# GpSimd adds the weights for the seven products, which cover all four column groups; operands at constant places mod 256

## The chip, the cores and the metric

One core of a Trainium2 chip runs the whole program. The metric is device time in microseconds (us), lower is better. Engines: TensorE (PE; PEld is its weight load), VectorE (DVE), ScalarE (ACT), GpSimd (POOL), and SyncE (SP), which issues the loads.

## The reference

One decoder layer in fp32: a sequence of 256 tokens behind 16 meta tokens, model width 2048, MLP width 8192.

```python
u = rmsnorm(h, g_mix);  proj = u @ w_in          # 2048 -> 6144
o_diff = diff_attention(...);  o_sb = stick_breaking_attention(...)
h = h + concat(o_diff, o_sb) @ w_out              # 2048 -> 2048
m = rmsnorm(h, g_mlp)
hid = square(relu(m @ w_up))                      # 2048 -> 8192
h = h + hid @ w_down                              # 8192 -> 2048
```

## The kernel before

**Products.** Each fp32 product is made of three matmuls in a rounded format (fp32r): hi x hi, hi x lo and lo x hi, where hi is the rounded value and lo the rest. `triple` issues the three. A weight tile comes from memory as a *raw* tile, 128 x 4 x 256 fp32 (512 KB), on SP's queue, into one of five raw buffers. ACT casts it (`whi`, L179) and DVE subtracts (`wlo`, L181). The results go into weight buffers, of which the MLP has five, used in turn along `order`: the split of item g waits until item g - 5 has been used by PE. The split runs four items ahead.

**The MLP.** The hidden width is cut into 8 rounds of 1024 columns. In a round, PE makes the hidden columns of the *next* round ("up", 16 items) and the share of the present one in the output ("down"). The output is 2048 wide, in four column groups u of 512; a *unit* (r, u) is one column group of one round, with four weight tiles p = 0 to 3. The letters in the code are items of PE's order:

- c: one up tile, 24 matmuls with 256 moving columns.
- d: one plain down tile, 12 matmuls of 512 columns.
- a and b: one down tile in the form with seven products in place of eight (a Strassen-like scheme on 2 x 2 blocks; the units in `FAST`). "a" makes three products from three quarters of the raw tile as they are (9 matmuls of 256, a cast and a subtraction of 768 wide). Then three additions overwrite parts of the raw tile with sums of its quarters (L295 with 512 columns, L297 and L299 with 256, all on DVE). "b" makes four products from the summed tile (12 matmuls of 256, split 1024 wide). A raw tile is free when b is split.

The seven products of a column group are summed over all rounds: at the end of a fast unit ACT copies the four PSUM banks to `Z[u]` (L930), and copies the next unit's `Z` back into its banks (L935) where one exists, bank by bank in the order 0, 1, 3, 2 (`fast_evac`; bank 3 is half-sized). At the last fast round of a column group its seven sums are combined. A plain unit's result is added to H by DVE (`plain_evac`). The hidden values need block sums of their own (three DVE operations in `up_evac`, L887 to L891), after ACT's relu and square; then they are cast (ACT, L897) and subtracted (DVE, L899) 1024 wide.

**What sets the order.** PE's order is the list `order`: for each round a string per column group. ACT's, DVE's and SP's instructions are written down by a planner, `Pace`, which keeps a model clock for each engine and lets a job go on when its inputs are there by that clock and the engine is at most 500 ns ahead of PE; each engine then runs its own list in that order, waiting where an input is late. Before, column groups 0, 1 and 2 are fast in rounds 0 to 6, and the four d of group 3 are spread over the units:

```python
for u, mix in ((0, "cdcabcabcabcab"), (1, "cdcabcabcabcab"), (2, "cdcabcabcdabccab")):
```

In the last round (no up left) only group 0 is fast.

**Places.** LINE is 16 fp32 (64 bytes). The pads and `offset` set at which address modulo 256 the operands lie: m, mixed, hid (moving or stationary) and the weight buffers' hi and lo.

Of the kernel before, what the change touches and what calls it, by code (L numbers as in the profile page):

```python
# [7 lines left out]
F32 = mybir.dt.float32  # L8
F32R = mybir.dt.float32r
AF = mybir.ActivationFunctionType  # L10
ALU = mybir.AluOpType
AX = mybir.AxisListType

P = 128
DM = 2048
SEQ = 256
META = 16
TOK = META + SEQ
KT = DM // P
EPS = 1e-6  # L20
NEG = -1e30
ROW = 576
LINE = 16
ROUNDS = 8
PAIRS = 4
# [5 lines left out]
MLP_PARTS = 5  # L31
MLP_LEAD = 4
MLP_PAD = 1
FAST = {(r, u) for r in range(ROUNDS - 1) for u in range(3)} | {(ROUNDS - 1, 0)}
PSUM_BANKS = {"acc": 4, "att": 4}
SLOTS = {"k": 4, "q": 4, "v": 2, "e": 3, "pr": 2, "ah": 2, "m": 2, "n": 2}
K0 = META + P
# [8 lines left out]
class Pace:  # L46
# [9 lines left out]
    QUEUE = 500.0  # L56

    def __init__(self, lanes):
        self.pe = self.dve = self.act = 0.0
        self.lanes = {n: ([], w) for n, w in lanes}  # L60
        self.at = {}
        self.banks = {}
# [9 lines left out]
    def A(self, n, after=0.0):  # L72
        self.act = max(self.act, self.pe, after) + n / 1.2 + 93
        return self.act + self.WAIT

    def job(self, lane, gen):
        self.lanes[lane][0].append([(0.0, None), gen])
# [16 lines left out]
    def pump(self):  # L94
        more = True
        while more:
            more = False
            for jobs, width in self.lanes.values():
                for job in jobs[:width]:
                    t, engine = job[0]  # L100
                    if t <= self.pe and {None: 0, "v": self.dve, "a": self.act}[engine] <= self.pe + self.QUEUE:
                        try:
                            job[0] = next(job[1])
                        except StopIteration:
                            jobs.remove(job)
                        more = True
                        break
                if more:
                    break
# [13 lines left out]
def hymba_layer(ctx: ExitStack, tc: tile.TileContext, xT_d, xh_d, win_d, wout_d, wup_d, wdn_d, cst_d, par_d, out_d):  # L123
    nc = tc.nc
    cp = ctx.enter_context(tc.tile_pool(name="const", bufs=1))
    big = ctx.enter_context(tc.tile_pool(name="big", bufs=1))
    wp = ctx.enter_context(tc.tile_pool(name="weights", bufs=1))
# [7 lines left out]
    pc = Pace((("fetch", 9), ("weights", 9), ("once", 2), ("evac", 6), ("head", 4)))  # L135
# [17 lines left out]
    def retile(tag, shape, name):  # L153
        return rtile(tag, shape, name, SLOTS["e"])

    def two_parts(x, k, n):

        return x[:, :, : k * n].rearrange("p a (k n) -> p k a n", n=n)


    par = cp.tile([P, G_END], F32, name="par")
    cst = tp.tile([P, C_ID], F32, bufs=1, name="cst")
# [1 line left out]
    xT = big.tile([P, KT, TOK], F32, tag="x", name="xT")  # L164
    big.tile([P, LINE], F32, name="pad_act")
    um = big.tile([P, KT, ROW], F32R, tag="act", name="u")[:, :, : 2 * TOK].rearrange("p k (a n) -> p k a n", a=2)
    big.tile([P, 2 * LINE], F32, name="pad_mix")
    mixed = two_parts(big.tile([P, 2, KT * SEQ + LINE], F32R, tag="mix", name="mixed"), KT, SEQ)

    def split_u(k):  # L170
        g = par[:, G_MIX + k : G_MIX + k + 1]
# [13 lines left out]
    strips = []  # L185
# [16 lines left out]
    def down(r, u, ps):  # L202
        return [(x, r, u, p) for p in ps for x in ("ab" if (r, u) in FAST else "a")]

    order += up(0, 0, range(3)) + up(0, 1, range(3)) + up(0, 0, (3,)) + up(0, 1, (3,)) + up(0, 2, range(4)) + up(0, 3, range(4))
    for r in range(ROUNDS - 1):
        c = iter([key for i in range(PAIRS) for key in up(r + 1, i, range(4))])
        d = iter(down(r, 3, range(PAIRS)))
        for u, mix in ((0, "cdcabcabcabcab"), (1, "cdcabcabcabcab"), (2, "cdcabcabcdabccab")):
            ab = iter(down(r, u, range(PAIRS)))  # L210
            order += [next({"c": c, "d": d, "a": ab, "b": ab}[x]) for x in mix]
        assert not [*c, *d]
    ab = iter(down(ROUNDS - 1, 0, range(PAIRS)))
    d = iter([key for u in (1, 2, 3) for key in down(ROUNDS - 1, u, range(PAIRS))])
    order += [next({"d": d, "a": ab, "b": ab}[x]) for x in "dd" + "adbd" * 4 + "dd"]
# [20 lines left out]
    def fetch(number, pieces=1):  # L236
        if number < len(loads):
            g = loads[number]
            if not raws:
                wp.tile([P, 3 * LINE], F32, name="pad_w")  # L240
            raws[g] = wp.tile([P, 4, 256], F32, tag="raw", bufs=RAW, name=f"raw_{g}")
            n = 4 // pieces
            for i in range(pieces):
                k = slice(n * i, n * i + n)
                raw_at[g, i] = load(raws[g][:, k], source(g)[:, k], n * 256)
                yield

    ring = {g: g - PARTS for g in range(len(order))}

    def offset(g):  # L250

        what, *at = order[g]
        if what == "in":
            return LINE if strips[at[0]][1] in (0, 3) else 0
        return LINE if what == "up" and at[1:] in ([0, 0], [2, 0]) else 0  # L260

    def part(g, pieces=1):
        if g < len(order) and g not in parts:
            pool, bufs, tag = wp, PARTS, "w"
            if g >= first_mlp:
                ring[g] = max(g - MLP_PARTS, first_mlp - PARTS + (g - first_mlp) % MLP_PARTS) if (g - first_mlp) % MLP_PARTS < PARTS else g - MLP_PARTS
                if (g - first_mlp) % MLP_PARTS >= PARTS:
                    pool, bufs, tag = mp, MLP_PARTS - PARTS, "v"
                    ring[g] = ring[g] if g - MLP_PARTS >= first_mlp else -1
            at = offset(g)  # L270
            hi, lo = (
                pool.tile([P, 1024 + 4 * LINE], F32R, tag=tag + x, bufs=bufs, name=f"w{x}_{g}")[:, n : n + 1024]
                .rearrange("p (k n) -> p k n", k=4)
                for x, n in (("hi", at), ("lo", at + LINE))
            )
            parts[g] = (hi, lo)
            what, *at = order[g]
            fast = what in "ab" and (at[0], at[1]) in FAST
            pc.job("weights", (fast_a if what == "a" else fast_b)(g, hi, lo) if fast else halves(g, hi, lo, pieces))

    def fast_a(g, hi, lo):

        while (g, 0) not in raw_at or ring[g] >= 0 and ring[g] not in done_at:
            yield pc.pe + 200, None
        yield max(raw_at[g, 0], done_at.get(ring[g], 0.0)), "a"
        raw = raws[g]  # L290
        t = yield from split(hi[:, 1:4], lo[:, 1:4], raw[:, 1:4], 768)
        for kk in range(4):
            pc.at["w", g, kk] = t
        first = raw[:, 0:1].to_broadcast([P, 2, 256])
        nc.vector.tensor_tensor(raw[:, 3::-3], first, raw[:, 3:1:-1], op=ALU.add)  # L295
        pc.V(512)
        nc.vector.tensor_tensor(raw[:, 2], raw[:, 3], raw[:, 2], op=ALU.add)  # L297
        pc.V(256)
        nc.vector.tensor_tensor(raw[:, 1], raw[:, 2], raw[:, 1], op=ALU.add)  # L299
        pc.at["sums", g] = pc.V(256)  # L300

    def fast_b(g, hi, lo):
        while ("sums", source_of[g]) not in pc.at or ring[g] >= 0 and ring[g] not in done_at:
# [22 lines left out]
    g = 0  # L326
    for c in range(4):
        n = 2 if c == 0 else 4
# [474 lines left out]
    m = H = mp = None  # L803
# [52 lines left out]
    def mtile(tag, shape, name, bufs=1, dt=F32):  # L856
        return mp.tile(shape, dt, tag=tag, bufs=bufs, name=name)
# [2 lines left out]
    hid, Z = {}, {}  # L860

    def hidden(r):
        if r == 1:
            mp.tile([P, 3 * LINE], F32, name="pad_hid")
        if r % 2:
            x = mtile("hid", [P, 2, PAIRS * FULL * P + LINE], f"hid_{r}", 1, F32R)
        else:
            x = big.tile([P, 2, KT * SEQ + LINE], F32R, tag="mix", name=f"hid_{r}")
        hid[r] = two_parts(x, PAIRS * FULL, P).rearrange("p (q s) a n -> p q s a n", q=PAIRS)

    def up_evac(r, i, o):

# [197 lines left out]

    def triple(out, x, w, first, last, check=False):

        for i, (a, b) in enumerate(((1, 0), (0, 0), (0, 1))):
            nc.tensor.matmul(  # L1074
                out, lhsT=x[a], rhs=w[b], start=first and i == 0, stop=last and i == 2, skip_group_check=check
            )
        n = out.shape[-1]
        return pc.T(3 * (n / 2.4 + 2.5))

    for g in range(index["out", 0, 0], first_mlp):  # L1080
        _, u, c = order[g]
        if c == 0:
            out = banks("acc", 2, f"out_{u}")
            if u == 0:
                m = big.tile([P, KT, ROW], F32R, tag="act", name="m")[:, :, : 2 * TOK].rearrange("p k (a n) -> p k a n", a=2)[:, :, :, :SEQ]
        if u == 1 and c == 0:
            while pc.lanes["head"][0] or any(("mixed", k) not in pc.at for k in range(KT)):
                pc.pe += 100
                pc.pump()
            attention.close()  # L1090
            mp = ctx.enter_context(tc.tile_pool(name="mlp", bufs=1))
            mp.tile([P, MLP_PAD * LINE], F32, name="pad_mlp")
        begin(g, LEAD)
        hi, lo = (x.rearrange("p (k a) b -> p k (a b)", k=2) for x in parts[g])
        for kk in range(2):
            k = 2 * c + kk
            pc.stall(("w", g, 2 * kk + 1), ("mixed", k))
            for i in range(2):
                x = [mixed[:, k, a, P * i : P * i + P] for a in range(2)]
                t = triple(out[i], x, (hi[:, kk], lo[:, kk]), k == 0, k == KT - 1)  # L1100
                pc.pump()
        done_at[g] = pc.pe
        if c == 7:
            pc.job("evac", after(t, out_evac(u, out)))
            if u == 3:
                pc.job("once", mlp_norm())
# [111 lines left out]
```

## Time and profile before

| | |
|---|---|
| runs, device us | 1131.67 median of three (1131.6 to 1132.87) |
| profiled execution | 1131.64, span 1129.87 |
| PE's granted clock over the span | 1.00 |
| busy: PE, PEld, DVE, ACT, POOL | 99%, 95%, 84%, 71%, 0% |
| PE instructions | 8599 |
| DMA | 210.00 MB, 186 GB/s, all tiles on SP's queue |
| chain that ended last | PE 97%, of which up 32%, down 28%, the in-projection's acc 24%, out 8% |
| rounds of the MLP (windows of 86.1 us) | PE 86.1, DVE 76.1, ACT 61.9 busy |

The rounds are read between first "up" matmuls of successive rounds; round 1 is 573.26 to 659.37. In the rows of groups, what stands behind the idle time (`<-`) names what ended it.

### The profile page before, as it was taken

To read this page: it belongs to the slowest core of one execution; us is meant where nothing else is said; L and a number is where in the kernel's file an instruction comes from. 1 tells how busy PE (TensorE), PEld (TensorE's weight loads), DVE (VectorE), ACT (ScalarE), POOL (GpSimd) and SP (SyncE) were. 2 spreads that over 40 slices of the span, in tenths; PEclk is the share of its full clock that TensorE was granted. 3 is DMA by queue.
4 is the path that set the end of the run, shared out by engine and by line. 5 is a ranking of instruction groups with operands and counts; after the bars stand their busy time and mean duration, and the time that the engine had idled before them with its cause. 6 is when DMAs were issued, how large, how long until landed. Compare 5 with 4: busy or idle time off the path is not lost.

```text
span 1129.9 us, 21823 instructions
## 1 busy us (share of the span) xinstructions
PE 1121.4 (99%) x8599; PEld 1075.7 (95%) x8599; DVE 947.2 (84%) x1459; ACT 798.4 (71%) x1283; POOL 1.1 (0%) x8
## 2 busy tenths in 40 slices
PE   8999999999999999999999999999999999999998
PEld 7999999999998889999999999999999999999987
DVE  6988988888876556698898899888889888888997
ACT  7779888788776445566577677677677677777663
POOL 0000000000000000000000000000000000000000
PEclk9999999999999999999999999999999999999999
DMA  8564544555545556555556555555555655655653
GB/s 332 185 225 133 156 143 150 150 162 154 156 148 171 182 187 212 180 179 194 196 187 207 190 186 199 200 189 190 203 187 195 215 187 187 222 183 193 209 179 135
DMA packets 58134, 210.00 MB, mean 186 GB/s; under 512 B 6576, under 2 KB 6832, under 8 KB 57904
## 3 DMA queue, kind: packets, MB, share of 16 engines
q1 hardware_dynamic: 58032, 208.61, 56.2%
q8 instruction: 67, 1.10, 0.4%
q14 instruction: 35, 0.29, 0.1%
HBM read 206.49 MB, written 2.10 MB: 185 GB/s over the span
## 4 chain that ended last, share of the span: by engine, by line
PE 97%; DMA 1%; ACT 1%; SPq 0%; DVE 0%; issue 0%; ACTq 0%
PE up L1068 32%; PE down L1074 28%; PE acc L983 8%; PE acc L985 8%; PE acc L984 8%; PE out L1074 8%; DMA xT<-in_x 1%; PE s_d L630 1%; PE po_s L670 1%; PE po_d L670 1%; PE z_s L630 1%; SPq L232 0%; PE pt L834 0%; PE pq_dq L558 0%; ACT whi L179 0%
## 5 line engine op out<-in xcount | busy, mean ns | idle before, releaser
L181 DVE TENSOR_TENSOR wlo<-raw,whi 128x1024 fp32r<-128x1024 f32 (+2 forms) x478 | 539.5, 1158 | 117.0 <-ACT whi L179 115.4
L179 ACT CAST whi<-raw 128x1024 fp32r<-128x1024 f32 (+2 forms) x478 | 466.2, 998 | 215.9 <-PE up L1068 63.2
L1068 PE MATMUL up<-m,whi 128*128 128x256 f32 x2048 | 366.6, 279 | 0.0
L1074 PE MATMUL down<-whi,hid 128*128 128x256 f32 (+1 forms) x1552 | 321.7, 304 | 0.7 <-ACT down L935 0.7
L1068 PEld LDWEIGHTS up<-m,whi 128*128 128x128 f32 x2048 | 314.9, 188 | 2.0
L1068 PE MATMUL up<-m,wlo 128*128 128x256 f32 x1024 | 287.0, 280 | 0.0
L1074 PEld LDWEIGHTS down<-whi,hid 128*128 128x128 f32 x1552 | 246.4, 188 | 13.5 <-ACT down L935 0.9
L1074 PE MATMUL down<-wlo,hid 128*128 128x256 f32 (+1 forms) x776 | 234.6, 302 | 0.0
L983 PE MATMUL acc<-u,whi 128*128 128x272 f32 (+1 forms) x768 | 222.4, 290 | 1.4 <-ACT whi L179 1.4
L985 PE MATMUL acc<-u,wlo 128*128 128x272 f32 (+1 forms) x768 | 219.0, 285 | 1.2 <-DVE wlo L181 1.2
L984 PE MATMUL acc<-u,whi 128*128 128x272 f32 (+1 forms) x768 | 217.4, 283 | 0.0
L1068 PEld LDWEIGHTS up<-m,wlo 128*128 128x128 f32 x1024 | 192.3, 188 | 0.0
L1074 PEld LDWEIGHTS down<-wlo,hid 128*128 128x128 f32 x776 | 145.5, 188 | 7.1
L983 PEld LDWEIGHTS acc<-u,whi 128*128 128x128 f32 x768 | 144.4, 188 | 3.0 <-ACT whi L179 2.1
L985 PEld LDWEIGHTS acc<-u,wlo 128*128 128x128 f32 x768 | 144.2, 188 | 1.8 <-DVE wlo L181 1.8
L984 PEld LDWEIGHTS acc<-u,whi 128*128 128x128 f32 x768 | 144.4, 188 | 0.0
L1074 PE MATMUL out<-whi,mixed 128*128 128x512 f32 x256 | 80.8, 397 | 0.0
L295 DVE TENSOR_TENSOR raw<-raw 128x512 f32<-128x512 f32 x88 | 60.9, 692 | 3.0
L1074 PEld LDWEIGHTS out<-whi,mixed 128*128 128x128 f32 x256 | 47.2, 188 | 10.1
L1074 PE MATMUL out<-wlo,mixed 128*128 128x512 f32 x128 | 50.5, 394 | 0.0
L879 ACT ACTIVATE hx<-up 128x512 f32<-128x512 f32 x32 | 19.1, 596 | 44.1 <-PE up L1068 44.1
L930 ACT COPY z<-down 128x512 f32<-128x512 f32 (+1 forms) x88 | 45.8, 528 | 3.0 <-PE down L1074 3.0
(241 smaller groups left out, 918.8 us busy)
## 6 DMA issues: line engine op xcount, KB each, us to landing
raw<-in_wup SPq DMA_DIRECT2D x128, 512.0 KB, 4.6
raw<-in_wdn SPq DMA_DIRECT2D x128, 512.0 KB, 3.7
raw<-in_win SPq DMA_DIRECT2D x95, 512.0 KB, 3.6
raw<-in_wout SPq DMA_DIRECT2D x32, 512.0 KB, 3.5
H<-in_xh SPq DMA_DIRECT2D x1, 2048.0 KB, 8.2
out<-H SPq DMA_DIRECT2D x8, 256.0 KB, 2.0
xT<-in_x SPq DMA_DIRECT2D x3, 544.0 KB, 9.8
cst<-in_cst SPq DMA_DIRECT2D x1, 609.0 KB, 11.0
```

Of the source, the lines that this page charges most:

```text
L179: nc.scalar.copy(hi, src)
L181: nc.vector.tensor_tensor(lo, src, as32(hi), op=ALU.subtract)
L295: nc.vector.tensor_tensor(raw[:, 3::-3], first, raw[:, 3:1:-1], op=ALU.add)
L630: nc.tensor.matmul(dst, lhsT=q[x][rows, cols], rhs=k[y][rows, :n], start=i == 0, stop=i == 2)
L670: nc.tensor.matmul(o, lhsT=l, rhs=r, start=i == 0, stop=i == len(todo) - 1)
L879: nc.scalar.activation(x[:, 0:4].rearrange("p a b -> p (a b)"), o, AF.Relu)
L930: nc.scalar.copy(Z[u][:, at], o[i][:, :n])
L983: nc.tensor.matmul(o, lhsT=h, rhs=xh, start=first, stop=False)
L984: nc.tensor.matmul(o, lhsT=h, rhs=xl, start=False, stop=False)
L985: nc.tensor.matmul(o, lhsT=l, rhs=xh, start=False, stop=last)
L1068: nc.tensor.matmul(out, lhsT=w[a], rhs=x[:, b], start=first and i == 0, stop=last and i == 2, skip_group_check=True)
L1074: nc.tensor.matmul(out, lhsT=x[a], rhs=w[b], start=first and i == 0, stop=last and i == 2, skip_group_check=check)
```

## The change

1. **All four column groups are fast** in rounds 0 to 6: 29 fast units in place of 22, 116 summed raw tiles in place of 88. Every unit of these rounds has the same string, "ccababcabcab": 4 c, 4 a, 4 b. A fourth `Z` tile exists.
2. **The sums move from DVE to GpSimd**: 348 additions, with a planner's clock for that engine (`G`).
3. **Places**: `offsets` gives hi and lo their places apart, mixed and hid hold hi and lo of one block side by side, m is packed, and pads change. From the tiles' addresses: after, the moving operands of up, down and out lie at 224 mod 256 and the stationary ones at 160 (two up tiles of a round at 224). Before, up's moving operands lay at 224 (hi) and 32 (lo) with stationary at 160 and 224, those of down and out at 160 and 224 with stationary at 160 and 96.
4. **The order in a triple**: hi x hi first.

```diff
-FAST = {(r, u) for r in range(ROUNDS - 1) for u in range(3)} | {(ROUNDS - 1, 0)}
+FAST = {(r, u) for r in range(ROUNDS - 1) for u in range(4)} | {(ROUNDS - 1, 0)}
...
+    def G(self, n):
+        self.pool = max(self.pool, self.pe) + n / 0.45 + 100
+        return self.pool + self.WAIT
...
-    mixed = two_parts(big.tile([P, 2, KT * SEQ + LINE], F32R, tag="mix", name="mixed"), KT, SEQ)
+    mixed = big.tile([P, KT, 2, SEQ], F32R, tag="mix", name="mixed")
...
-        for u, mix in ((0, "cdcabcabcabcab"), (1, "cdcabcabcabcab"), (2, "cdcabcabcdabccab")):
+        for u in range(4):
             ab = iter(down(r, u, range(PAIRS)))
-            order += [next({"c": c, "d": d, "a": ab, "b": ab}[x]) for x in mix]
+            order += [next({"c": c, "a": ab, "b": ab}[x]) for x in "ccababcabcab"]
...
         what, *at = order[g]
         if what == "in":
-            return LINE if strips[at[0]][1] in (0, 3) else 0
-        return LINE if what == "up" and at[1:] in ([0, 0], [2, 0]) else 0
+            line = strips[at[0]][1] in (0, 3)
+            return line * LINE, line * LINE + LINE
+        line = at[1:] in ([0, 0], [2, 0]) if what == "up" else at != [0, 0] if what == "out" else True
+        return line * LINE, line * LINE
...
+        yield t, "g"
         first = raw[:, 0:1].to_broadcast([P, 2, 256])
-        nc.vector.tensor_tensor(raw[:, 3::-3], first, raw[:, 3:1:-1], op=ALU.add)
-        pc.V(512)
-        nc.vector.tensor_tensor(raw[:, 2], raw[:, 3], raw[:, 2], op=ALU.add)
-        pc.V(256)
-        nc.vector.tensor_tensor(raw[:, 1], raw[:, 2], raw[:, 1], op=ALU.add)
-        pc.at["sums", g] = pc.V(256)
+        nc.gpsimd.tensor_tensor(raw[:, 3::-3], first, raw[:, 3:1:-1], op=ALU.add)
+        pc.G(512)
+        nc.gpsimd.tensor_tensor(raw[:, 2], raw[:, 3], raw[:, 2], op=ALU.add)
+        pc.G(256)
+        nc.gpsimd.tensor_tensor(raw[:, 1], raw[:, 2], raw[:, 1], op=ALU.add)
+        pc.at["sums", g] = pc.G(256)
...
-            x = mtile("hid", [P, 2, PAIRS * FULL * P + LINE], f"hid_{r}", 1, F32R)
+            hid[r] = mtile("hid", [P, PAIRS, FULL, 2, P], f"hid_{r}", 1, F32R)
...
-        for i, (a, b) in enumerate(((1, 0), (0, 0), (0, 1))):
+        for i, (a, b) in enumerate(((0, 0), (1, 0), (0, 1))):
```

The place of the prediction's main term is the start of a fast unit; the rows below are those around unit (3, 1). The number after `whi`, `wlo` and `raw` is the item's place in `order`; after an "a" its "b" is the next number. Before, 293 and 294 are the last a and b of unit (3, 0), 295 a c, 296 and 297 an a and a b of unit (3, 1). On ACT before, the copies follow the cast of the old unit's last a:

```order
L179 CAST whi_293_9694<-raw_293_9581 128x768
L930 COPY z_0_6611<-down_3_0_0_9385 128x512
L935 COPY down_3_1_0_9718<-z_1_6937 128x512
L930 COPY z_0_6611<-down_3_0_1_9401 128x512
L935 COPY down_3_1_1_9731<-z_1_6937 128x512
L930 COPY z_0_6611<-down_3_0_3_9419 128x256
L935 COPY down_3_1_3_9743<-z_1_6937 128x256
L930 COPY z_0_6611<-down_3_0_2_9463 128x512
L935 COPY down_3_1_2_9752<-z_1_6937 128x512
L179 CAST whi_294_9710<-raw_293_9581 128x1024
```

After, unit (3, 1) has the items 300 and 301 (c), 302 to 305 (a, b, a, b), 306 (c), 307 and 308 (a, b), 309 (c), 310 and 311 (a, b); 312 is the next unit's. On ACT:

```order
L179 CAST whi_304_9863<-raw_304_9742 128x768
L926 COPY z_0_6557<-down_3_0_0_9603 128x512
L931 COPY down_3_1_0_9880<-z_1_6832 128x512
L893 CAST hid_4_9892<-hx_4_0_9842 128x8x128
L926 COPY z_0_6557<-down_3_0_1_9629 128x512
L931 COPY down_3_1_1_9907<-z_1_6832 128x512
L179 CAST whi_303_9847<-raw_302_9782 128x1024
L926 COPY z_0_6557<-down_3_0_3_9654 128x256
L931 COPY down_3_1_3_9932<-z_1_6832 128x256
L926 COPY z_0_6557<-down_3_0_2_9664 128x512
L931 COPY down_3_1_2_9942<-z_1_6832 128x512
L179 CAST whi_305_9909<-raw_304_9742 128x1024
```

The copies now stand behind the cast of the unit's second a, and a cast of hidden values and the first b's cast between them. Behind the last row the casts of 306, 307, 309, 310 and 308 follow. On DVE before, a subtraction of an a and its three sums stood together:

```order
L181 TENSOR_TENSOR wlo_296_9772<-raw_296_9652,whi_296_9771 128x768
L295 TENSOR_TENSOR raw_296_9652<-raw_296_9652 128x2x256
L297 TENSOR_TENSOR raw_296_9652<-raw_296_9652 128x256
L299 TENSOR_TENSOR raw_296_9652<-raw_296_9652 128x256
L181 TENSOR_TENSOR wlo_298_9819<-raw_298_9684,whi_298_9818 128x1024
```

After, DVE has subtractions alone there, with that of b 308 three places behind its a's:

```order
L181 TENSOR_TENSOR wlo_305_9910<-raw_304_9742,whi_305_9909 128x1024
L181 TENSOR_TENSOR wlo_306_9945<-raw_306_9804,whi_306_9944 128x1024
L181 TENSOR_TENSOR wlo_307_9961<-raw_307_9806,whi_307_9960 128x768
L181 TENSOR_TENSOR wlo_309_9993<-raw_309_9836,whi_309_9992 128x1024
L181 TENSOR_TENSOR wlo_310_10011<-raw_310_9946,whi_310_10010 128x768
L181 TENSOR_TENSOR wlo_308_9981<-raw_307_9806,whi_308_9980 128x1024
```

and POOL, which had eight instructions in all, has the sums of the same raw tiles:

```order
L294 TENSOR_TENSOR raw_304_9742<-raw_304_9742 128x2x256
L296 TENSOR_TENSOR raw_304_9742<-raw_304_9742 128x256
L298 TENSOR_TENSOR raw_304_9742<-raw_304_9742 128x256
L294 TENSOR_TENSOR raw_307_9806<-raw_307_9806 128x2x256
L296 TENSOR_TENSOR raw_307_9806<-raw_307_9806 128x256
L298 TENSOR_TENSOR raw_307_9806<-raw_307_9806 128x256
```

The sums of an a left DVE's list for POOL's, and start when DVE's subtraction of that a has ended.

More of the change, by code (lines that the diff above doesn't have):

```diff
@@ L58, in __init__ @@
     def __init__(self, lanes):
-        self.pe = self.dve = self.act = 0.0
+        self.pe = self.dve = self.act = self.pool = 0.0
         self.lanes = {n: ([], w) for n, w in lanes}
@@ L100, in pump @@
                     t, engine = job[0]
-                    if t <= self.pe and {None: 0, "v": self.dve, "a": self.act}[engine] <= self.pe + self.QUEUE:
+                    if t <= self.pe and {None: 0, "v": self.dve, "a": self.act, "g": self.pool}[engine] <= self.pe + self.QUEUE:
                         try:
@@ L154, in retile @@
         return rtile(tag, shape, name, SLOTS["e"])
-    def two_parts(x, k, n):
-        return x[:, :, : k * n].rearrange("p a (k n) -> p k a n", n=n)
     par = cp.tile([P, G_END], F32, name="par")
@@ L166, in hymba_layer @@
     um = big.tile([P, KT, ROW], F32R, tag="act", name="u")[:, :, : 2 * TOK].rearrange("p k (a n) -> p k a n", a=2)
-    big.tile([P, 2 * LINE], F32, name="pad_mix")
-    mixed = two_parts(big.tile([P, 2, KT * SEQ + LINE], F32R, tag="mix", name="mixed"), KT, SEQ)
+    big.tile([P, 3 * LINE], F32, name="pad_mix")
+    mixed = big.tile([P, KT, 2, SEQ], F32R, tag="mix", name="mixed")
     def split_u(k):
@@ L207, in hymba_layer @@
         c = iter([key for i in range(PAIRS) for key in up(r + 1, i, range(4))])
-        d = iter(down(r, 3, range(PAIRS)))
-        for u, mix in ((0, "cdcabcabcabcab"), (1, "cdcabcabcabcab"), (2, "cdcabcabcdabccab")):
+        for u in range(4):
             ab = iter(down(r, u, range(PAIRS)))
-            order += [next({"c": c, "d": d, "a": ab, "b": ab}[x]) for x in mix]
-        assert not [*c, *d]
+            order += [next({"c": c, "a": ab, "b": ab}[x]) for x in "ccababcabcab"]
+        assert not [*c]
     ab = iter(down(ROUNDS - 1, 0, range(PAIRS)))
@@ L238, in fetch @@
             g = loads[number]
-            if not raws:
-                wp.tile([P, 3 * LINE], F32, name="pad_w")
             raws[g] = wp.tile([P, 4, 256], F32, tag="raw", bufs=RAW, name=f"raw_{g}")
@@ L248, in hymba_layer, with offsets @@
     ring = {g: g - PARTS for g in range(len(order))}
-    def offset(g):
+    def offsets(g):
         what, *at = order[g]
         if what == "in":
-            return LINE if strips[at[0]][1] in (0, 3) else 0
-        return LINE if what == "up" and at[1:] in ([0, 0], [2, 0]) else 0
+            line = strips[at[0]][1] in (0, 3)
+            return line * LINE, line * LINE + LINE
+        line = at[1:] in ([0, 0], [2, 0]) if what == "up" else at != [0, 0] if what == "out" else True
+        return line * LINE, line * LINE
     def part(g, pieces=1):
@@ L269, in part @@
                     ring[g] = ring[g] if g - MLP_PARTS >= first_mlp else -1
-            at = offset(g)
             hi, lo = (
@@ L273, in part @@
                 .rearrange("p (k n) -> p k n", k=4)
-                for x, n in (("hi", at), ("lo", at + LINE))
+                for x, n in zip(("hi", "lo"), offsets(g))
             )
@@ L862, in hidden @@
     def hidden(r):
-        if r == 1:
-            mp.tile([P, 3 * LINE], F32, name="pad_hid")
         if r % 2:
-            x = mtile("hid", [P, 2, PAIRS * FULL * P + LINE], f"hid_{r}", 1, F32R)
+            hid[r] = mtile("hid", [P, PAIRS, FULL, 2, P], f"hid_{r}", 1, F32R)
         else:
-            x = big.tile([P, 2, KT * SEQ + LINE], F32R, tag="mix", name=f"hid_{r}")
-        hid[r] = two_parts(x, PAIRS * FULL, P).rearrange("p (q s) a n -> p q s a n", q=PAIRS)
+            hid[r] = big.tile([P, PAIRS, FULL, 2, P], F32R, tag="mix", name=f"hid_{r}")
     def up_evac(r, i, o):
@@ L1084, in hymba_layer @@
             if u == 0:
-                m = big.tile([P, KT, ROW], F32R, tag="act", name="m")[:, :, : 2 * TOK].rearrange("p k (a n) -> p k a n", a=2)[:, :, :, :SEQ]
+                m = big.tile([P, KT, ROW], F32R, tag="act", name="m")[:, :, : 2 * SEQ].rearrange("p k (a n) -> p k a n", a=2)
         if u == 1 and c == 0:
```

## The prediction

> **What bounds the kernel now.** I read the page first (its busy line and the chain that ended last), then the chain as a list and the windows of single rounds, then the weights' own rows on ACT, DVE and PE. From the page:
>
> ```profile
> PE 1121.4 (99%) x8599; PEld 1075.7 (95%) x8599; DVE 947.2 (84%) x1459; ACT 798.4 (71%) x1283; POOL 1.1 (0%) x8
> PE 97%; DMA 1%; ACT 1%; SPq 0%; DVE 0%; issue 0%; ACTq 0%
> ```
>
> TensorE is the bound; POOL does nothing. The windows of rounds 1 and 5 of the MLP (start, end, then busy time by engine) show a machine without a hole in it:
>
> ```profile
> 573.26:659.37 86.11, 86.11 (x686) 83.93 (x685) 76.08 (x99) 61.85 (x80) 0.00 (x0) 1.00 0.59 195
> ...
> 917.71:1003.83 86.12, 86.12 (x687) 83.94 (x685) 76.00 (x99) 61.80 (x80) 0.00 (x0) 1.00 0.60 197
> ```
>
> PE is busy for all 86.11 us of a round, at clock 1.00, with DVE at 76 and ACT at 62. Pieces of the chain (start, length, how many matmuls) give what an item of the order costs:
>
> ```profile
> 774.95 2.83 PE up L1068 x24
> 777.78 2.47 PE down L1074 x21
> ...
> 793.68 2.80 PE down L1074 x12
> ```
>
> A "c" (24 matmuls of 256) is 2.83, an "a" with its "b" (9 + 12) is 2.47, so 1.06 + 1.41, and a "d" (12 of 512) is 2.80. Check: 16 x 2.83 + 12 x 2.47 + 4 x 2.80 = 86.1.
>
> **The gain: fewer columns.** Unit 3 of rounds 0 to 6 goes from four d (11.20) to four ab (9.88): 1.32 a round, 7 x 1.31 = 9.1 us off PE, all of it on the path as long as PE stays the bound. A round is then 84.8, a unit 21.2.
>
> **What the path needs beside PE.** A "b" is ready only after its "a" was cast (ACT), subtracted (DVE), its raw tile summed three times, cast again and subtracted again. First the rows of one execution of rounds 1 to 5, by form (mean ns in the middle):
>
> ```profile
> L181 DVE TENSOR_TENSOR wlo<-raw,whi 128x1024 fp32r<-128x1024 f32 x160 | 189.1, 1221 | 35.7 <-ACT whi L179 34.6
> L179 ACT CAST whi<-raw 128x1024 fp32r<-128x1024 f32 x160 | 162.2, 1048 | 78.7 <-PE up L1068 31.9 <-PE down L1074 22.2 <-DVE raw L299 20.4
> L181 DVE TENSOR_TENSOR wlo<-raw,whi 128x768 fp32r<-128x768 f32 x61 | 58.2, 953 | 2.3 <-ACT whi L179 2.3
> L179 ACT CAST whi<-raw 128x768 fp32r<-128x768 f32 x60 | 50.1, 835 | 10.8 <-PE down L1074 6.1 <-issue 3.3
> L899 DVE TENSOR_TENSOR hid<-hx,hid 128x1024 fp32r<-128x1024 f32 x20 | 24.4, 1218 | 0.0
> L897 ACT CAST hid<-hx 128x1024 fp32r<-128x1024 f32 x20 | 20.9, 1044 | 0.0
> ```
>
> Then three stretches of the timeline: two casts back to back on ACT, three subtractions and the sums on DVE, and the copies at a unit's end on ACT (start, length):
>
> ```profile
> 785.28 2.00 ACT L179 CAST whi<-raw 128x1024 fp32r<-128x1024 f32 x2 [1.22 <-DVE raw L299]
> ```
>
> ```profile
> 774.54 3.23 DVE L181 TENSOR_TENSOR wlo<-raw,whi 128x1024 fp32r<-128x1024 f32 x3 [1.19 <-ACT whi L179]
> 777.80 0.69 DVE L295 TENSOR_TENSOR raw<-raw 128x512 f32<-128x512 f32 x1
> 778.53 0.42 DVE L297 TENSOR_TENSOR raw<-raw 128x256 f32<-128x256 f32 x1
> 778.99 0.43 DVE L299 TENSOR_TENSOR raw<-raw 128x256 f32<-128x256 f32 x1
> 779.33 0.42 DVE L887 TENSOR_TENSOR hx<-hx 128x256 f32<-128x256 f32 x1
> ...
> 780.32 3.22 DVE L181 TENSOR_TENSOR wlo<-raw,whi 128x1024 fp32r<-128x1024 f32 x3
> ```
>
> ```profile
> 763.27 0.58 ACT L930 COPY z<-down 128x512 f32<-128x512 f32 x1
> 763.88 0.59 ACT L935 COPY down<-z 128x512 f32<-128x512 f32 x1
> 764.41 0.58 ACT L930 COPY z<-down 128x512 f32<-128x512 f32 x1
> ...
> 765.55 0.36 ACT L930 COPY z<-down 128x256 f32<-128x256 f32 x1
> 765.94 0.38 ACT L935 COPY down<-z 128x256 f32<-128x256 f32 x1
> 766.26 0.58 ACT L930 COPY z<-down 128x512 f32<-128x512 f32 x1
> ```
>
> Two casts take 2.00, not 2.10: in a row one costs 0.95 (0.74 for 768). Three subtractions (1.22 + 1.22 + 0.95) take 3.23: 1.14 each in a row (0.87 for 768). The sums take 1.62 (777.80 to 779.42). A z copy with its copy back costs 1.14, the half-sized pair 0.71.
>
> How close it is today: the tightest b that I found, its subtraction on DVE and its first matmul on PE.
>
> ```profile
> 787.38 1.22 DVE L181 TENSOR_TENSOR wlo<-raw,whi 128x1024 fp32r<-128x1024 f32 x1
> ```
>
> ```profile
> 789.28 0.28 PE L1074 MATMUL down<-whi,hid 128*128 128x256 f32 x1
> ```
>
> 0.68 us of slack (788.60 to 789.28). The change takes more than that.
>
> **The cost: the third b of a unit.** Count from the end of a unit, as the new order of ACT stands. ACT's cast of the second a (w304) needs the weight buffer of the b that has just ended, so it starts at +0.1, and the copies stand behind it (before, they began 0.6 ahead of the unit's end). Then, without a gap: cast a 0.74, pair 1.14, hid 0.95, pair 1.14, cast b303 0.95, small pair 0.71, pair 1.14, cast b305 0.95, cast c306 0.95, cast a307 0.74: a307 is cast at +9.5. DVE has the subtractions of b305 (starts at 7.9), c306 and a307 in a row: 7.9 + 1.14 + 1.14 + 0.95 = 11.2. Then POOL's three adds, 2.4 (below): 13.6. Cast of b308 1.05: 14.7; subtraction 1.22: 16.0; its lo half is first used two matmuls in, so PE may start b308 at 15.7. PE gets there at 2.83 x 3 + 2.47 x 2 + 1.06 = 14.5. Late by 1.2. The other b's and the copied sums of the next unit keep 0.2 to 0.6. Round 0 copies nothing back (2.1 us less on ACT ahead of a307) and isn't late; the 24 units of rounds 1 to 6 are: 24 x 1.2 = +28.8 us. Each unit's lateness ends with it, since ACT's chain starts anew at a unit's end.
>
> POOL's adds are not in the trace. From below, they take what DVE's took, 1.62: late by 0.45, +11 in all. From above, POOL's own rows:
>
> ```profile
> L468 POOL MEMSET stack_m<- 80x256 f32 x2 | 0.6, 308 | 0.3 <-POOLq L1210 0.3
> L468 POOL MEMSET stack_v<- 80x128 f32 x2 | 0.3, 202 | 0.0
> ```
>
> (308 - 202) / 128 = 0.83 ns an element and 0.1 us fixed; two reads and a write, one after the other, for 1024 elements in three instructions: 2.85, late by 1.65, +40. I take 2.4, nearer to POOL's own rows than to DVE's. The Trainium skill (GPSIMD Engine Reference, 3.1 Elementwise) gives 4497 ns for an add of 2048 elements; an estimate from it is 2.25 for the three, and the sum would be 3.6 us lower. No run here shows it yet.
>
> **The other edits.**
> - DVE loses 12 x 1.54 of sums in a round and POOL gains 16 sources; DVE was not waited for, so this alone earns nothing. SP's loads stay 32 a round. A raw tile is held until its b is subtracted: a310's comes back 6.3 + 3.7 (the median landing of in_wdn) + about 0.6 = 10.6, when its cast is up at 10.4. At most 0.2, and not on b308's chain.
> - The library row and the first add on POOL: ahead of the MLP, once; zero to some us, taken at zero.
> - Places mod 256 and hi*hi first: up and down have different places today and cost the same per matmul (2.83 / 24 = 0.118, 2.47 / 21 = 0.118). Zero is my value. For the bounds, one stage at constant places ran at two paces, 11.44 / 49 = 0.2335 and 9.22 / 40 = 0.2305:
>
> ```profile
> 352.05 11.44 PE out L1074 x49
> ```
>
> ```profile
> 374.58 9.22 PE out L1074 x40
> ```
>
>   1.3% of some 510 us of matmuls whose places move is 7 us, up or down.
> - The tail: the sums of unit 3 are combined once at the end of round 6, where unit 2's were; two or three DVE operations' worth at most.
>
> **Sum**, against the profiled execution's own 1131.64 (span 1129.87 and 1.77 around it; the median of the runs is 1131.67): 1131.6 - 9.1 + 28.8 = 1151.3.
>
> **The rivals.**
> 1. *POOL and DVE hinder each other.* In the new kernel every DVE instruction of a unit reads two SBUF operands while POOL reads two more; no row of the trace has the two reading together, so it can't say. For it: nothing shown. Against it: casts and subtractions on the same raw tiles run side by side today and keep to one length. If they take turns, a unit needs DVE's 8 x 1.14 + 4 x 0.87 + 1.14 + 0.99 (779.33 to 780.32) = 14.7 and POOL's 4 x 2.4 = 9.6, together 24.3 against PE's 21.2: 28 x 3.1 = +87, 1209 at the least. With the waits in the chain of b308 (three adds that each wait out a subtraction, two subtractions that wait out an add, 1 to 2.5 us) it is 25 to 27, so 1229 to 1285; I price it at 1250. It decides as soon as DVE and POOL together exceed 21.2. If they only slow each other by a sixth to a half, b308 is late by 2 to 3: 1165 to 1220. The Trainium skill has this rule (SBUF — State Buffer, Who interferes with whom): a DVE instruction with two SBUF inputs and a GpSimd instruction that reads SBUF share a read interface, and the second to start waits for the first to end. By that rule the change loses about 10%.
> 2. *Faster.* If the adds take 1.2 us or less a source, b308 is in time and all 9.1 us are kept: 1122.5. Break-even is 9.1 / 24 = 0.38 late, adds of 1.55, under DVE's own 1.62. So it needs a POOL faster than DVE, or a cheaper place for the operands besides.
> 3. *No change*: the same with adds near 1.55.
>
> **How the numbers follow.** This kernel's runs can tell about 0.2% (2.3 us) from no change. b308 late and no hindrance, 1135 to 1166: 0.42, the likeliest single case, hence 1151. Hindrance in part (1166 to 1220): 0.12. Full turns (1220 to 1285): 0.27, less than the case without them, since nothing in the rows speaks for it. Over 1285: 0.02. Faster: 0.13, since the margin of b308 is read from a chain of ten steps, each good to about a tenth of a us. Within 0.2%: 0.04. So slower has 0.83. The range leaves out these two and the slowest: 1138 to 1285. The forecast's own range is 1138 to 1166.
>
> **What would show it.** Right: PE waits at the first matmuls of "down" for DVE wlo or ACT whi, about once a unit and 1 to 1.4 us, from round 1 on and not in round 0; rounds of 89 to 90 us; POOL's adds near 1.2 and 0.6; DVE's 1221 and ACT's 1048 unchanged. Hindrance: DVE's 1221 grows or its starts slip behind POOL, POOL's spans stretch to 2 us, and round 0 is late as well. Faster: rounds of 84.8 and no waits. Pace: pieces of 24 or 21 matmuls that are not 2.83 or 2.47. I am wrong most easily by POOL: its speed and its company.

## The result, and the profile after

The changed kernel takes 1300.17 us (median of four runs, 1299.22 to 1300.78) against 1131.63 for the kernel before on the same chip: ratio 1.1486, 95% interval 1.1466 to 1.1506. The forecast was 1151.3 with a range up to 1285. The direction was forecast, the size was not: it was the rival with GpSimd and DVE in turns, and beyond its upper end.

The page of the changed kernel, its busy line and the shares of the chain that ended last:

```profile
PE 1188.9 (92%) x8851; PEld 1131.5 (87%) x8851; DVE 985.8 (76%) x1220; ACT 842.1 (65%) x1363; POOL 466.4 (36%) x356
PE 51%; POOL 18%; DVE 15%; ACT 9%; issue 6%; DMA 0%; SPq 0%; DVEq 0%; POOLq 0%; ACTq 0%
```

TensorE falls from 97% of that chain to 51%; GpSimd, DVE and ACT take 42%. TensorE's waits (total us, times, longest):

```profile
PE down L1070 <- ACT whi L179: 63.4, 29, 3.6
PE down L1070 <- DVE wlo L181: 39.2, 82, 1.5
```

The windows: round 2, the first unit of round 3, then in that unit the idle stretch ahead of its third b, and a stretch of 3.41 us that starts soon after it (the last columns are granted clock, DMA share and GB/s):

```profile
693.90:803.84 109.94, 95.41 (x723) 91.34 (x721) 81.04 (x65) 68.64 (x93) 64.05 (x49) 0.94 0.47 153
803.84:831.18 27.34, 23.73 (x182) 22.71 (x181) 20.25 (x17) 17.12 (x24) 16.01 (x13) 0.94 0.49 153
819.90:822.06 2.16, 0.00 (x1) 0.00 (x1) 0.02 (x1) 1.10 (x2) 2.08 (x3) 1.00 0.33 131
822.79:826.20 3.41, 2.88 (x13) 2.89 (x14) 2.14 (x2) 0.81 (x2) 2.65 (x2) 0.50 0.48 153
```

A round is 109.94 in place of 86.11. A unit is 27.34, where before a round's quarter was 21.53. TensorE is busy for 23.73 of it. So 3.6 a unit is idle time, and 2.5 is busy time above the 21.2 forecast. Part of this is the clock: 0.73 us after the wait's end it falls to 0.50, for 3.41 us, which costs at most 1.7 us a unit. The rest of the 2.5 was not taken apart. 28 x 3.6 = 101 agrees with the 102.6 of waits; 28 x 2.5 = 70 is what the longer busy time comes to.

The rows by form (mean ns before: 1221, 1219, 422 for the three of DVE):

```profile
L181 DVE TENSOR_TENSOR wlo<-raw,whi 128x1024 fp32r<-128x1024 f32 x378 | 488.5, 1312 | 225.8 <-ACT whi L179 223.0 <-PE down L1070 2.5
L895 DVE TENSOR_TENSOR hid<-hx,hid 128x1024 fp32r<-128x1024 f32 x32 | 63.9, 1998 | 8.3 <-ACT hid L893 8.3
L883 DVE TENSOR_TENSOR hx<-hx 128x256 f32<-128x256 f32 x32 | 39.9, 1248 | 5.0 <-ACT hx L879 5.0
L294 POOL TENSOR_TENSOR raw<-raw 128x512 f32<-128x512 f32 x116 | 183.3, 1580 | 797.0 <-DVE wlo L181 793.7 <-DMA raw<-in_wdn 3.3
L296 POOL TENSOR_TENSOR raw<-raw 128x256 f32<-128x256 f32 x116 | 150.9, 1300 | 9.1
L298 POOL TENSOR_TENSOR raw<-raw 128x256 f32<-128x256 f32 x116 | 132.4, 1141 | 9.1
```

Identical instructions grew where the two engines meet. How they meet shows in the timeline of one unit, GpSimd first, then DVE:

```profile
803.35 1.30 POOL L294 TENSOR_TENSOR raw<-raw 128x512 f32<-128x512 f32 x1 [5.21 <-DVE wlo L181]
804.73 0.81 POOL L296 TENSOR_TENSOR raw<-raw 128x256 f32<-128x256 f32 x1
805.61 0.74 POOL L298 TENSOR_TENSOR raw<-raw 128x256 f32<-128x256 f32 x1
807.45 1.29 POOL L294 TENSOR_TENSOR raw<-raw 128x512 f32<-128x512 f32 x1 [1.10 <-DVE wlo L181]
808.82 1.60 POOL L296 TENSOR_TENSOR raw<-raw 128x256 f32<-128x256 f32 x1
810.50 1.59 POOL L298 TENSOR_TENSOR raw<-raw 128x256 f32<-128x256 f32 x1
```

```profile
803.48 1.46 DVE L883 TENSOR_TENSOR hx<-hx 128x256 f32<-128x256 f32 x1 [0.20 <-ACT hx L879]
...
807.62 2.20 DVE L895 TENSOR_TENSOR hid<-hx,hid 128x1024 fp32r<-128x1024 f32 x1 [0.25 <-ACT hid L893]
809.75 1.76 DVE L181 TENSOR_TENSOR wlo<-raw,whi 128x1024 fp32r<-128x1024 f32 x1
```

Read it as a queue of two. GpSimd's add runs from 807.45 to 808.74; DVE's subtraction was issued at 807.62 and ends at 809.82, 1.08 after the add. The next add was issued at 808.82 and ends at 810.42, 0.60 after that subtraction. DVE's next ends at 811.51, 1.09 after that add, and the last add at 812.09, 0.58 after it. Each starts to work when the other has ended. The whole trace says the same: 27 of the 32 subtractions of hidden values (L895) were issued while an add ran, and all 27 end 1.080 to 1.085 after that add, while the five others take 1.22. Of the 232 adds of 256 columns, 197 were issued behind one DVE instruction that still ran, and they end 0.58 to 0.67 after it.

### The profile page after: what moved, and what is told of

Its sections match the earlier page's. It is cut to its first block, busy times and chain, and to the rows that moved or that the text cites. A ratio compares the mean times of both kernels' runs of the same rounds, so it can differ in the third digit from the quotient of the medians.

```text
span 1299.0 us, 22710 instructions
## 1 busy us (share of the span) xinstructions
PE 1188.9 (92%) x8851; PEld 1131.5 (87%) x8851; DVE 985.8 (76%) x1220; ACT 842.1 (65%) x1363; POOL 466.4 (36%) x356
## 3 DMA queue, kind: packets, MB, share of 16 engines
q8 instruction: 69, 1.13, 0.3%
## 4 chain that ended last, share of the span: by engine, by line
PE 51%; POOL 18%; DVE 15%; ACT 9%; issue 6%; DMA 0%; SPq 0%; DVEq 0%; POOLq 0%; ACTq 0%
PE up L1064 10%; DVE wlo L181 9%; PE down L1070 8%; PE acc L979 7%; PE acc L981 7%; POOL raw L294 7%; PE acc L980 7%; PE out L1070 7%; ACT whi L179 6%; POOL raw L296 6%; POOL raw L298 5%; DVE hx L883 3%; DVE hx L885 2%; ACT hx L879 1%; ACT hx L875 1%
## 5 line engine op out<-in xcount | busy, mean ns | idle before, releaser
L181 DVE TENSOR_TENSOR wlo<-raw,whi 128x1024 fp32r<-128x1024 f32 (+2 forms) x506 | 626.6, 1268 | 254.8 <-ACT whi L179 251.7
L179 ACT CAST whi<-raw 128x1024 fp32r<-128x1024 f32 (+2 forms) x506 | 484.1, 987 | 355.5 <-POOL raw L298 218.4
L294 POOL TENSOR_TENSOR raw<-raw 128x512 f32<-128x512 f32 x116 | 183.3, 1580 | 797.0 <-DVE wlo L181 793.7
L1070 PE MATMUL down<-whi,hid 128*128 128x256 f32 (+1 forms) x1720 | 349.7, 300 | 64.9 <-ACT whi L179 63.4
L1070 PEld LDWEIGHTS down<-whi,hid 128*128 128x128 f32 x1720 | 281.4, 199 | 79.4 <-ACT whi L179 69.5
L1064 PEld LDWEIGHTS up<-m,whi 128*128 128x128 f32 x2048 | 331.4, 199 | 0.1
L1070 PE MATMUL down<-wlo,hid 128*128 128x256 f32 (+1 forms) x860 | 267.4, 311 | 39.3 <-DVE wlo L181 39.2
L1070 PEld LDWEIGHTS down<-wlo,hid 128*128 128x128 f32 x860 | 172.9, 201 | 58.5 <-DVE wlo L181 56.5
L296 POOL TENSOR_TENSOR raw<-raw 128x256 f32<-128x256 f32 x116 | 150.9, 1300 | 9.1
L298 POOL TENSOR_TENSOR raw<-raw 128x256 f32<-128x256 f32 x116 | 132.4, 1141 | 9.1
L895 DVE TENSOR_TENSOR hid<-hx,hid 128x1024 fp32r<-128x1024 f32 x32 | 63.9, 1998 | 8.3 <-ACT hid L893 8.3
```

The source lines that it names most:

```text
L179: nc.scalar.copy(hi, src)
L181: nc.vector.tensor_tensor(lo, src, as32(hi), op=ALU.subtract)
L294: nc.gpsimd.tensor_tensor(raw[:, 3::-3], first, raw[:, 3:1:-1], op=ALU.add)
L296: nc.gpsimd.tensor_tensor(raw[:, 2], raw[:, 3], raw[:, 2], op=ALU.add)
L298: nc.gpsimd.tensor_tensor(raw[:, 1], raw[:, 2], raw[:, 1], op=ALU.add)
L895: nc.vector.tensor_tensor(lo, x, as32(hi), op=ALU.subtract)
```

## The experiments

Three theories stood after this. T: GpSimd's adds and DVE's two-operand instructions take turns. R1: the new order of a, b and c makes the waits. R2: GpSimd's adds are only too long for the chain of the third b.

**Who adds, and the order.** `sums_dve`: the additions back on DVE.

```diff
-        yield t, "g"
-        nc.gpsimd.tensor_tensor(...)  # three times
+        nc.vector.tensor_tensor(...)
```

> The changed kernel with the sums on DVE again; four fast groups, order of the items and places stay. Theory T (a GpSimd add and a DVE operation with two SBUF operands exclude each other for the whole instruction): a unit needs 14.7 + 4 x 1.62 = 21.2 of DVE against 21.2 of PE, so units of 21.5 to 23.5 and 1131 to 1187, 1150 likeliest; the hidden values' subtraction back at 1.22. Rival R1 (the new order of a, b and c makes the waits, whoever adds): units of 27 stay, 1280 or more. Rival R2 (only the length of GpSimd's adds): 1122 to 1140.

Measured 1178.81 (ratio 1.0426, 1.0408 to 1.0443). 121 of the 168 us went with the adds' engine and with the other order that the planner then gave ACT and DVE. It is inside T's band. But what is left was not the DVE bound that T gave: TensorE waited for the copies at a unit's start.

```profile
PE down L1069 <- ACT down L930: 31.8, 49, 1.3
```

The string "cc" leaves 5.65 us for them, where "cdc" had left 8.4. `no_sums` leaves out the three additions.

> The changed kernel without the three additions (b is split from the tile as loaded, so b's products are of other weights); GpSimd idle. It gives the gain of the columns and of the places alone. T and R2: 1122.5 (1118 to 1128), units of 21.2. R1: waits stay, over 1200.

Measured 1157.38 (1.0225, 1.0208 to 1.0242): a miss for T and R2, whose 1122.5 was to be the gain alone, and under R1's 1200 as well.

```profile
PE down L1063 <- ACT down L924: 29.0, 49, 1.0
```

49 waits again: ACT's list has two casts of tiles needed later between the second and the third pair of a unit's copies. So R1 holds in part: the new order of items, with the lists that the planner makes from it, is 26 us over the kernel before even with no sums at all.

`before_pool`: the kernel before, the sums on GpSimd, nothing else.

> The kernel before with the sums on GpSimd and nothing else changed (three fast groups, its order, its places). T: a round needs 76.1 - 12 x 1.54 = 57.6 of DVE and 12 x 2.9 = 34.8 of GpSimd, 92.4 together against 86.1: 1176 at the least, up to 1230 with the waits in the chains; the hidden values' subtraction grows from 1.22 to about 2. R1: 1131, within 10. R2: the tightest b loses 1.3 against a slack of 0.68, 1131 to 1180, and DVE's durations stay as they were.

Measured 1197.42 (1.0584, 1.0568 to 1.06), in the band of T and out of those of R1 and R2. DVE's and GpSimd's rows:

```profile
L894 DVE TENSOR_TENSOR hx<-hx 128x128 f32<-128x128 f32 x32 | 24.4, 762 | 1.1
...
L904 DVE TENSOR_TENSOR hid<-hx,hid 128x1024 fp32r<-128x1024 f32 x32 | 40.6, 1269 | 7.2 <-ACT hid L902 6.9
...
L300 POOL TENSOR_TENSOR raw<-raw 128x512 f32<-128x512 f32 x88 | 131.9, 1498 | 852.2 <-DVE wlo L185 843.5 <-DMA raw<-in_wdn 8.7
```

The expected row missed: the hidden values' subtraction is 1.27, since it seldom meets an add there; the small subtraction ahead of it met one, and went from 292 to 762 ns.

**Is it the reading?** `pool_writes` replaces each add by a write.

```diff
-        nc.gpsimd.tensor_tensor(raw[:, 3::-3], first, raw[:, 3:1:-1], op=ALU.add)
...
+        for i in range(3):
+            nc.gpsimd.memset(raw[:], 1.0)
```

> The changed kernel with each of GpSimd's three adds replaced by a write of the whole raw tile (1024 elements, some 0.95 us each by GpSimd's rows of before, 2.85 for the three, as long as the three adds take when DVE is idle): GpSimd reads nothing, the chain through it keeps its length. T, if it is the reads that exclude: DVE's durations are 1.22, 0.42 and 0.2 again, the third b of a unit is late by 1 to 2, 1150 to 1190. If any GpSimd instruction excludes DVE: 1280 or more with DVE's durations stretched. R2: as the changed kernel, 1290 to 1300, with DVE's durations unstretched.

Measured 1161.74 (1.0267, 1.0252 to 1.0283).

```profile
L181 DVE TENSOR_TENSOR wlo<-raw,whi 128x1024 fp32r<-128x1024 f32 x378 | 454.5, 1222 | 204.8 <-ACT whi L179 204.2
L891 DVE TENSOR_TENSOR hid<-hx,hid 128x1024 fp32r<-128x1024 f32 x32 | 39.2, 1225 | 25.4 <-ACT hid L889 25.4
...
L294 POOL MEMSET raw<- 128x1024 f32 x348 | 329.0, 955 | 808.3 <-DVE wlo L181 794.9
```

This is inside T's 1150 to 1190, and far under the 1280 or more and the 1290 to 1300 of the two others. GpSimd is as long in the chain (3 x 0.955 = 2.87), writes while DVE works, and DVE's rows are those of before to a few ns. ACT's 1363 and DVE's 1220 instructions stand in the same order in this trace and in the changed kernel's, so the planner's order is not what differs. So 1300.2 - 1161.7 = 138 us is what the turns cost with all that follows from them. The Trainium skill (SBUF — State Buffer, Who interferes with whom) says that a DVE instruction with two SBUF inputs contends with a GpSimd one that reads SBUF and not with one that only writes. Both halves agree with this pair of runs. The pair doesn't part the reads from the adding itself: a copy on GpSimd, with one read and one write, was not run. The b's also multiply other numbers here, at a granted clock of 1.000.

**Distance from a to b.** `late_b_pool` has "cacabcabcabb" in place of "ccababcabcab".

> The changed kernel with the string "cacabcabcabb" for every unit: each b two or more items behind its a, in place of right behind it. T (GpSimd and DVE take turns, so that 14.7 of DVE and 4 x 2.9 of GpSimd fill 26.3 of a unit): at best 28 x (27.4 - 26.3) = 31 less, 1269 to 1295. Rival R1 (the waits come from the short way from a to b): 1150 to 1200.

Measured 1319.08 (1.1656, 1.1639 to 1.1673): more room between a and b doesn't help, against R1, but it isn't T's 1269 to 1295 either. The waits moved:

```profile
PE down L1070 <- ACT down L931: 84.9, 49, 3.3
```

Here it is the first a of a unit that waits, for ACT's copies. `copies_first_dve` puts the copies ahead in the planner, with the sums on DVE (in the MLP, the job lane "evac" before "weights").

> The kernel with the sums on DVE (1178.8) and the planner, in the MLP, putting ACT's copies of the sums ahead of its casts. There TensorE waited 31.8 us in 49 waits for the copies ahead of a unit's first a, 5.65 us behind the unit's start, where the kernel before left 8.4. If this is the rest of the loss: 1178.8 - 32 = 1147, or less down to 1122.5 if b's keep in time; if the casts that now stand behind the copies come late in turn: 1165 to 1200.

Measured 1310.12 (1.1575, 1.1558 to 1.1593), a plain miss: the waits for copies went, and the longest chain of a unit then ran through DVE, which had later tiles' subtractions and sums written ahead of the second b's subtraction (94.9 us of waits for it, in 35). The order that the planner finds at these loads is worth as much as the engine choice.

**TensorE's clock.** `filler` issues the third a's 9 matmuls twice more in each unit, inside the long wait.

```diff
+                if what == "a" and p == 2 and r < ROUNDS - 1:
+                    for at, half, slot, q in 2 * todo:
+                        triple(..., False, False, True)
```

> The changed kernel with the 9 matmuls of the third a of each unit of rounds 0 to 6 issued three times (its products count threefold in the sums). The 18 added ones take 18 x 0.118 = 2.1 us and stand where TensorE idles 2.2 us for the third b; each engine's order is otherwise that of the changed kernel. Theory C (TensorE's granted clock falls for some 4 us because it idled): no long wait is left, the b and c behind run at 0.118 a matmul in place of up to 0.21, 28 x 1.2 = 34 us less, about 1266. Rival C1 (the matmuls behind the wait are slow for another reason, such as traffic in SBUF): 1300, within 8. Rival C2 (the added work is not in a wait): 1300 + 59 = 1359.

Measured 1275.89 (1.1274, 1.1255 to 1.1293). 28 x 2.1 = 59 us of work more, and the kernel is 24 us shorter. The span's mean granted clock went from 0.959 to 0.996:

```profile
core 0: 1275.2 us, clock 0.996
```

ACT's, DVE's and GpSimd's lists are those of the changed kernel. So it is shown that the clock falls because TensorE idled. The gain is 24 in place of 34; 45.2 us of waits for DVE's lo halves remained (39.2 before the filling), which is the likely reason and was not tested.

**Places.** `places`: the kernel before with the new places and the order in a triple, and no other part of the change.

> The kernel before with the changed kernel's places and order in a triple, and nothing else of the change (three fast groups, old order of items, sums on DVE). The stage out ran 384 matmuls in 93.6 us in place of 94.5 in the changed kernel; up and down keep 2.83 and 2.47. So 0.9 less, 1130.4 (1128 to 1134). If places matter for the MLP's matmuls too: up to 7 either way.

Measured 1110.44 (0.9815, 0.9801 to 0.983): 21 us faster than the kernel before, and the best of all here. Its rounds:

```profile
643.75:727.14 83.39, 83.39 (x687) 81.42 (x685) 75.95 (x99) 61.49 (x82) 0.00 (x0) 1.00 0.63 203
```

83.39 in place of 86.11, with the same matmuls: in the chain a c takes 2.72 in place of 2.83 and an a with its b 2.38 in place of 2.47. But constant places don't make this pace by themselves, as the next runs show. `places_old_triple` goes back to lo x hi first.

> The kernel 'places' with the old order of the three matmuls in down and out (lo x hi first). The up matmuls had hi x hi first in both kernels, and went from 0.1178 to 0.1133. If the addresses do it all: 1110.4, within 1.5. If down's share of the gain hangs on the order of the three: 1116 to 1122.

Measured 1110.66 (0.9819, 0.9806 to 0.9832): the order in a triple does nothing. `places_up160` moves the two up tiles of a round that lay at 224 to 160:

```diff
-        line = at[1:] in ([0, 0], [2, 0]) if what == "up" else ...
+        line = False if what == "up" else ...
```

> The kernel 'places' with the two up tiles of each round whose stationary operand lies at 224 moved to 160 like all others. In 'places' their 384 matmuls took 0.120 each, the others 0.1134: 384 x 0.0065 = 2.5 less, 1108 (1107 to 1109). If that place served the change from down to up: 1110 to 1113.

Measured 1128.14 (0.9972, 0.9961 to 0.9982), the other way: with all operands at constant places the whole MLP runs at the old pace.

```profile
649.32:735.22 85.90, 85.90 (x687) 83.93 (x686) 76.02 (x99) 61.75 (x81) 0.00 (x0) 1.00 0.59 196
```

So there are two paces for the same addresses, 0.118 and 0.1133 a matmul, and the two odd tiles of a round bring TensorE into the fast one. The trace of `no_sums`, which has these places and a clock of 1.000, shows them do it: of the 14 up tiles that stand right behind an odd one, 13 take 0.113 a matmul; in rounds 1 to 6 all up tiles behind the wait that follows take 0.118, until the next odd tile. `places_one_wait` disturbs `places` once:

```diff
+                if (r, u, i) == (2, 2, 0):
+                    for _ in range(12):
+                        nc.scalar.copy(new[i][:, :n], Z[u2][:, at])
```

> The kernel 'places' (1110.4) with one disturbance: at the end of unit (2, 2) ACT makes the first copy back into the next unit's bank 13 times in place of once (12 x 0.59 = 7.1 us once), so that TensorE waits 2 to 7 us there, once. Theory P (the fast pace of 0.113 a matmul is a state that a wait ends, and that doesn't come back by itself): the 365 us behind it are 4% longer, 1110 + 4 + 14 = 1128 (1122 to 1132). Rival P1 (pace hangs on the places alone): 1112 to 1118.

Measured 1119.37 (0.9897, 0.9884 to 0.9911), between the two. The chain behind the wait (which ended at 742.50):

```profile
748.57 2.47 PE down L1073 x21
751.04 2.83 PE up L1067 x24
...
761.64 2.83 PE up L1067 x24
764.47 2.76 PE down L1073 x12
767.23 2.72 PE up L1067 x24
769.95 2.38 PE down L1073 x21
```

The granted clock is 0.50 from 740.0 to 746.8, and 1.00 after it. There the pace is the slow one until 764.47, and the fast one comes back behind a plain d. Theory P had half of it: the wait ended the fast pace, but it does come back. A wait doesn't always end it: in `pool_writes`, at a clock of 1.000, the c behind the waits of one unit takes 2.72 (from 581.01 on) and behind those of the next 2.83 (from 604.01 on). In the changed kernel every unit has waits, so most items have 2.83 again. `places_in` puts the in-projection at constant places.

> The kernel 'places' with the in-projection at constant places too (hi and lo of u 1280 bytes apart in place of 1088; moving at 224 with stationary at 160, and 32 with 224 where the meta tokens are left out). Its 1536 matmuls of 272 columns took 0.124 on average, its 768 of 256 0.118. If constant places make the pace there as in the MLP: 2304 x 0.0046 = 10.6 less, 1100 (1098 to 1104). If it is something of the MLP: 1110, within 1.5.

Measured 1113.79 (0.9844, 0.9831 to 0.9858): a miss, 3.4 us slower than `places`. Constant places without something that sets the fast pace gave nothing there.

## Why the prediction was wrong, by its steps

- **What bounds the kernel**: right; TensorE alone, until the change took more than the slack.
- **The gain of 9.1 us from fewer columns**: never seen by itself. Without any sums the new order ran 1157, 35 above the 1122.5, and 29.0 of it were waits for the copies at a unit's start. The step "the copied sums of the next unit keep 0.2 to 0.6" held in the changed kernel (no wait for them in its list), and not in its neighbours.
- **The third b is late**: the place was right. It has the longest waits, and the chain through it is the one that I walked. The chain as the list of waits has it, from the subtraction of the third a on:

```profile
815.48 0.96 DVE wlo L181
816.45 0.07 issue
816.51 2.22 POOL raw L294
...
818.80 1.33 POOL raw L296
...
820.21 0.73 POOL raw L298
...
820.96 1.05 ACT whi L179
822.01 0.02 issue
822.04 1.24 DVE wlo L181
```

  From the unit's start (803.84): that subtraction ends at +12.6 (forecast 11.2), the adds at +17.1 (13.6), the cast at +18.2 (14.7), the last subtraction at +19.4 (16.0). The first 1.4 are turns too: ACT, ahead of it, stood 1.26 for a stretched DVE row and 0.64 for GpSimd's adds (its timeline, waits in brackets). The adds took 4.4 in place of 2.4.

```profile
806.53 1.05 ACT L893 CAST hid<-hx 128x1024 fp32r<-128x1024 f32 x1 [1.26 <-DVE hx L887]
...
812.12 3.68 ACT L179 CAST whi<-raw 128x1024 fp32r<-128x1024 f32 x4 [0.64 <-POOL raw L298]
```

- **GpSimd's own speed**: mis-sized. 2.4 was taken; adds that overlap no DVE instruction take 1.29 for 512 columns (34 of them in `before_pool`) and 0.72 for 256 (33 in the changed kernel). The three make 2.73, and 2.88 with the two gaps between them (0.07 and 0.08), as much as the upper bound of 2.85 from the memset rows. With that bound and no turns the working gave 1131.6 - 9.1 + 40 = 1162, and `pool_writes`, that very case, measured 1161.7. Its shape is the forecast one too: round 0 takes 86.4 there and the later ones about 91.3, 6.5 above the 84.8, or 1.6 a unit. That the sum agrees to 1 us is luck all the same, since places, at zero in it, are in the run.
- **The failed step is the overlap**: the sum lets GpSimd's adds run beside DVE's subtractions, each at its own length, and puts +28.8 for all that is late. The runs showed turns in its place: the adds against writes of the same length, with the same lists, cost 138 us (1300.17 against 1161.74). The turns had 0.27 as a rival, "less than the case without them, since nothing in the rows speaks for it". No row of the old trace could: GpSimd was idle throughout. The row held against it, casts and subtractions side by side, was ACT's company and not GpSimd's. The rule of the Trainium skill that the prediction quotes (SBUF — State Buffer, Who interferes with whom) spoke for it, and these runs bear it out. The weight belonged on that rival.
- **The price of that rival**: 25 to 27 a unit was forecast, 27.4 came. DVE's 14.7 and GpSimd's 4 x 2.85 make 26.1; the waits in series and the halved clock behind each long wait come on top. Neither the fall of the clock nor its 24 us or more was in any case of mine. The case of hindrance in part was summed loosely: late by 2 to 3 in 24 units is 1170 to 1195, not 1165 to 1220.
- **Places at zero, 7 at most**: wrong by 21 us where nothing disturbs TensorE. The two paces of the stage out, which I quoted, were a sign; I took them for a spread of 1.3%, where the MLP's two paces lie 4% apart.
- **What would show it**: right in the case of hindrance (DVE's rows stretch, GpSimd's spans reach 2, round 0 is late as well: 104.7 there).

The loss in one line: 138 us from the turns (with the clock that falls behind the long waits), the rest from adds of 2.85 in a chain with no room (`pool_writes`, 30 us over the kernel before, has 33 us of waits for the halves of down tiles and 0.4 for the copies), against gains of up to 21 from the places and 9 from the columns that the waits keep from showing.

## What to carry to other kernels

Before handing an idle engine some work, ask whether it shares a way to memory with the busy one: two-operand adds on GpSimd take DVE's time as well as their own, and a slower engine then holds the shared thing longer than the work took on DVE (2.88 us here for what took DVE 1.62). When a change has several parts, measure the dull one by itself: here the places alone are worth 1.9% in the kernel before, and were hidden under a loss of 15%. A new order with fewer items ahead of a unit's start needs its copies priced at that start.

## What the runs showed of the hardware that I had not expected

- The granted clock goes by stretches of 3.41 us. In the changed kernel it falls to 0.50 for one or two of them at a time, and in the MLP each fall comes a whole number of such stretches after the last. Cut the trace along this grid from 440 us on. TensorE's busy share was 8 to 52% in the 27 stretches at full clock that a half-clock one follows, and 57 to 100% in the 193 others. In `pool_writes`, where the clock stays 1.000, no stretch is under 56%. In the other traces the border lies between 47 and 52%. So the length of one wait doesn't decide it: two waits of 1.13 and 0.75 us in one stretch of round 0 were enough.

```profile
546.31:549.72 3.41, 1.53 (x11) 1.11 (x10) 1.88 (x2) 2.00 (x2) 3.26 (x3) 1.00 0.05 20
549.72:553.13 3.41, 3.41 (x19) 3.41 (x18) 1.72 (x2) 1.78 (x2) 1.59 (x1) 0.50 0.78 191
```

  The Trainium skill (TensorE: Matmul & The Clock Gate, Part 1: The HAM clock gate) has a gate that halves the clock after an idle window of some 3.4 us. The half and the 3.41 us agree; the window didn't have to be idle here, about half of it was enough.
- One and the same matmul at the same addresses has two paces, 0.1133 and 0.118 us. An odd tile (one of the two up tiles of a round at another place) brings in the fast one, and most waits end it. Why, and why a d brought it back in one run and none of them in `places_up160`, stays open. The new places also put hi and lo of a block side by side; that was not tried apart from the addresses.
- Which of the two paces the in-projection would take with odd tiles of its own wasn't tried.
